# Low parts of weights by adding DMAs, shifted rows for the context's pairs, first modulation in column groups

## Chip, cores and metric

One core of one Trainium2 chip runs the whole kernel. The metric is the device time of one execution in microseconds; the time before is the median of three runs.

## The reference, cut to what matters

Two layers of a hybrid block work on a sequence x of 512 positions and a context of 256 positions, both 1024 wide. Per layer a modulation vector is made from c (for x) and c_ctx (for the context), then each stream is normed, modulated and projected; four branches (retention, short convolution, conformer convolution, windowed attention) are gated and merged.

```python
m = silu(cvec) @ w_mod + b_mod; shift, scale, gate = split(m, 3)
h = rmsnorm(x, norm_w) * (1 + scale) + shift
p = h @ w_in                                   # 1024 -> 11008
r, s, f, a = retention, short conv, conformer conv, attention of p
merged = sum(sigmoid(gate_i) * (branch_i @ w_branch[i]))
x = x + gate * (merged @ w_out)
```

The last layer needs only keys, values and states of the context. After it x is normed once more.

## The kernel before

Everything is kept transposed: features on the 128 partitions, positions along the row, so a stream is 8 blocks (`KC`) of 128 x 512 (x) or 128 x 256 (context). Every large product is done in parts. An operand is split into a high part (rounded to fp32r by a ScalarE copy) and a low part (VectorE: value minus high part), and `mm3` adds three matmuls for each of the 8 blocks: high weight by high data, high weight by low data, low weight by high data. One weight chunk (1024 x 128) is therefore 24 matmuls, moving 256 columns for the context and 512 for x.

The order of work is context of layer 0 (c0), x of layer 0 (x0), keys and values of the context of layer 1 (c1), x of layer 1 (x1), `final`. Within a stream: 54 projection chunks, then 32 gate chunks, each with a branch chunk of 12 matmuls, then 8 output chunks (`mix_out`). TensorE's order is written out by hand; `Tally` holds a planner's costs per engine, and `slot` steps the side flows (retention, attention, convolution taps, norms) between the dense matmuls when the planner says that their inputs are due. The other engines' orders come from the scheduler.

Weights: `w_load` brings a chunk from HBM on SyncE's queue (two 256 KB halves into rows for the context, one 512 KB load into `wraw` for x), `w_split` makes its high and low part in one of three pairs of tiles (`wt`, named wh and wl in the trace), and `w_ahead` keeps two chunks split ahead. The branch weights go into rows of their own (r in the trace). In `w_split`:

```python
nc.scalar.activation(hi, raw, AF.Copy)
nc.vector.tensor_tensor(lo, raw, hi.bitcast(F32), op=ALU.subtract)
```

Rows: `Arena` has 59 rows of 2048 bytes, all starting at a multiple of 64 bytes, and 12 of half that size. Everything that lives longer than an instruction or two is in one: raw weights, activations, splits. A context pair (`pair`, h and l behind the number in the trace) has its two parts in the halves of one row.

Start: `start` does c0's modulation, norm and the first three projections before anything else runs. For each of the 8 blocks, `mod_pe` splits four 128 x 512 tiles of w_mod into high and low part and multiplies them with the four columns of `s4` (high and low of the two silu vectors), `mod_pe_end` adds the four rows and turns them into columns, `modulate` makes the pair of that block, and the dense matmuls of the block follow `LAG` = 3 blocks later.

Of the kernel before, what the change touches and what calls it, by code (L numbers as in the profile page):

```python
# [22 lines left out]
LAG = 3  # L23
# [93 lines left out]
    return c  # L117


NROWS = 59  # L120
PAD = 480


# [28 lines left out]
        self.ring = None  # L152


class Arena:


    def __init__(self, pool, n, nh):
        self.full = [pool.ring(2048, name=f"row{i}") for i in range(n)]
        self.half = [pool.ring(1024, name=f"hrow{i}") for i in range(nh)]  # L160
        self.n = 0

    def get(self, w, parts, keep, pair=False):
        free = self.half if keep and w <= 256 else self.full
        if not free:
            self.relief(free)
# [24 lines left out]
class Tally:  # L191
# [14 lines left out]
    def add(self, eng, op, a, k):  # L206
        aps = [x for x in (*a, *k.values()) if hasattr(x, "free_size")]
        out, src = aps[0], aps[1] if len(aps) > 1 else aps[0]
        n = src.free_size()
        ready = max([self.now, self.read.get(out.tensor.name, 0.0)] + [self.written.get(x.tensor.name, 0.0) for x in aps])  # L210
        if eng == "tensor":
            if op == "transpose":
                d = 0.109
            elif aps[2].dtype == F32:
                d = max(0.218, aps[2].free_size() / 600)
            else:
                d = aps[2].free_size() / 2400
                if aps[2].dtype == F32R and d < 0.1:
                    d = 0.213
            self.now += d  # L220
            end = self.now + 0.15
        else:
            if eng == "vector":
                d = 0.065 + n / 960
                if op in ("tensor_scalar", "tensor_copy") and n == src.free_size() and "PSUM" not in str(src.space):
                    d = 0.065 + n / 1920
            elif eng == "scalar":
                d = 0.1 + n / 1200
            elif eng == "gpsimd":
# [6 lines left out]
            if eng == "sync":  # L236
# [41 lines left out]
class Block:  # L278
    def __init__(self, ctx, tc, xc, vec, cst, w_a, w_g, w_b, w_o, w_m, out, out2):
# [3 lines left out]
        self.w_m = w_m  # L283

        rp = ctx.enter_context(tc.tile_pool(name="rp", bufs=1))
        rp.tile([P, PAD], F32, name="fill")
        self.arena = Arena(rp, NROWS, 12)
# [4 lines left out]
        self.wt = [[cp.tile([P, 1024], F32R, name=f"w{p}{i}") for p in "hl"] for i in range(3)]  # L292
# [4 lines left out]
        self.vec = cp.tile([P, NV], F32, name="vec")  # L297
# [6 lines left out]
        self.work = [pp.tile([P, 512], F32, name=f"k{i}") for i in range(4)]  # L304
        self.turn = {}
        self.wq, self.wraws, self.wready, self.wkeep = [], [], {}, {}
        self.lanes = [[] for _ in range(5)]
        self.turns = 0
        self.flow = None
# [72 lines left out]
    def get_banks(self, n):  # L382

        while True:
            i = self.turn.get("work", 0)
            ready = max(self.nc.over(self.work[(i + j) % 4]) for j in range(n))
# [38 lines left out]
    def w_load(self):  # L425
# [4 lines left out]
        if small:  # L430
            raws = [(self.row(), slice(o, o + 512)) for o in (0, 512)]
            for r, o in raws:
                nc.sync.dma_start(r.a, src[:, o])
            raws = [(r, r.a, o) for r, o in raws]
        else:
            raw = self.take("wraw")
            nc.sync.dma_start(raw, src)
            raws = [(None, raw, slice(0, 1024))]
        if kind == "g":
            r = self.row()  # L440
            nc.sync.dma_start(r.a, self.wsrc["b"][l, i])
            raws.append((r, r.a, None))
        self.wraws.append((key, raws))

    def w_split(self):
        nc = self.nc
        key, raws = self.wraws.pop(0)
        parts = [self.take("wt")]
        for _, raw, o in raws:
# [78 lines left out]
    def csilu(self):  # L528
# [9 lines left out]
        self.s4 = self.cp.tile([P, KC, 4], F32R, name="s4")  # L538
        nc.scalar.activation(self.s4[:, :, 0:2], self.cs, AF.Copy)
        nc.vector.tensor_tensor(self.s4[:, :, 2:4], self.cs, self.s4[:, :, 0:2].bitcast(F32), op=ALU.subtract)  # L540

    def mod_load(self, l, b, hs=range(4)):

# [12 lines left out]
            if 8 <= m < 16:  # L556
                nc.vector.tensor_scalar(o, o, 1.0, self.v(l, "nw", b, b + 1), op0=ALU.add, op1=ALU.mult)

    def mod_pe(self, tiles):
        nc = self.nc  # L560
        ps = self.bank_now()
        for h, t in enumerate(tiles):
            hi, lo = self.part(), self.part()
            nc.scalar.activation(hi.r, t.a, AF.Copy)
            nc.vector.tensor_tensor(lo.r, t.a, hi.a, op=ALU.subtract)
            for i, x in enumerate((hi, lo)):
                for k in range(2):
                    nc.tensor.matmul(ps[0:4, 0:256], self.s4[:, 2 * h + k], x.r[:, k * 256:k * 256 + 256],
                                     start=(h == 0 and i == 0 and k == 0), stop=(h == 3 and i == 1 and k == 1))
        return ps  # L570

    def mod_pe_end(self, l, b, ps):
        m4 = self.small("m4", [4, 256], 4)
        self.nc.scalar.activation(m4, ps[0:4, 0:256], AF.Copy)
        for j in range(2):
            self.nc.tensor.matmul(ps[:, 256 + 2 * j:258 + 2 * j], m4[:, cs(j)], self.c("sel")[0:4],
                                  start=True, stop=True)
        self.mod_add(l, b, ps[:, 256:], 2)

    def mod_flow(self, l, bs):  # L580
# [755 lines left out]
    def load_x(self, st):  # L1336
        return [self.load_row(st, k) for k in range(KC)]

    def load_row(self, st, k):

        o, w = (0, SEQ) if st.s == 0 else (SEQ, CTX)
        x = self.row(w)
        self.nc.sync.dma_start(x.a, self.xd[st.s][k] if st.l else self.xc[k, :, o:o + w])
        return x

    def start(self, st):

        nc = self.nc
        loads = [self.mod_load(0, 0)]
        st.x = self.load_x(st)  # L1350
        self.csilu()
        acc = None
        for k in range(KC):
            acc = self.square(st.x[k].a, acc)
        names = [("ak", 0), ("av", 0), ("ax", 0)]
        self.early = {}
        ws, pss = [], []
        mods = {}

        def dense(k):  # L1360
            for w, ps in zip(ws, pss):
                self.mm3(ps, w, [None] * k + [st.hx[k]] + [None] * (KC - 1 - k), ks=[k])

        for k in range(KC + LAG):
            if k + 1 < KC:
                loads.append(self.mod_load(0, k + 1))
            if k < 3:
                ws.append(self.w_get("a", st, CIDX[names[k]], False)[0])
                pss.append(self.take("dense")[:, :st.t])
                self.early[st, CIDX[names[k]]] = pss[-1]  # L1370
            if k < KC:
                mods[k] = self.mod_pe(loads.pop(0))
            if 1 <= k <= KC:
                self.mod_pe_end(0, k - 1, mods.pop(k - 1))
            if k == 1:
                res = []
                for _ in self.rms(acc, res):
                    pass
# [6 lines left out]
        st.x = st.rstd = None  # L1385

    def run(self):
        nc = self.nc
# [121 lines left out]
```

## Time and profile before

| | us |
|---|---|
| median of 3 runs (1830.43 to 1831.96) | 1831.37 |
| the profiled execution, its own time | 1828.66 |
| its span in the profile | 1826.9 |

The profile is of one execution. PE is TensorE's matmul row, PEld its weight loads, DVE is VectorE, ACT ScalarE, POOL GpSimd, SP SyncE (SPq its queue of DMA issues). A matmul's record is longer than the distance to the next one, since matmuls are pipelined: the pace is read from start to start. "d<-r81h,wl" reads: output in the PSUM tile d, moving operand r81h, weights wl. The granted TensorE clock is given as a share of the full 2.4 GHz.

### The profile page before, as it was taken

The numbers are of one execution on the slowest core, as the hardware profiler recorded it, in microseconds if no ns is written. First come the engines' busy times: TensorE is split into PE (matmuls) and PEld (weight loads), VectorE is DVE, ScalarE is ACT, GpSimd is POOL, SyncE is SP. The second block draws the span as 40 slices with busy tenths as digits, with TensorE's granted clock in tenths as the row PEclk, the third lists the DMA queues.
The fourth block names the chain that finished last, engine by engine and source line by source line (L and its number), as shares of the span: only waits on it lengthen the run. The fifth ranks groups of instructions, "written<-read, shape, count | busy, mean of one in ns | idle before, by whom it ended". The sixth has DMA issues, their size and how long they took to land. (4 is left out here: it accounts for less than half of the span.)

```text
span 1826.9 us, 27582 instructions
## 1 busy us (share of the span) xinstructions
PE 1798.4 (98%) x10242; PEld 1562.3 (86%) x10242; DVE 1326.9 (73%) x2635; ACT 851.6 (47%) x1625; POOL 27.9 (2%) x34
## 2 busy tenths in 40 slices
PE   6999999999999999999999999999999999999998
PEld 4999999988888888888888889888888888888888
DVE  8899999884556669996998457447999866344445
ACT  6666765553554544423423246445534554323223
POOL 1000000000000000000000000000000000000000
PEclk9999999999999999999999999999999999999999
DMA  9646477743222222233555552322222232332233
GB/s 315 246 129 207 120 239 231 233 138 116 70 70 68 83 81 80 95 113 124 183 167 170 159 190 76 116 70 70 65 92 84 84 95 91 111 105 90 87 116 116
DMA packets 104135, 232.60 MB, mean 127 GB/s; under 512 B 12864, under 2 KB 19776, under 8 KB 104000
## 3 DMA queue, kind: packets, MB, share of 16 engines
q1 hardware_dynamic: 104000, 230.84, 39.1%
q8 instruction: 80, 1.31, 0.3%
q14 instruction: 55, 0.45, 0.1%
HBM read 218.73 MB, written 5.24 MB: 123 GB/s over the span
## 5 line engine op out<-in xcount | busy, mean ns | idle before, releaser
L187 PE MATMUL d<-r,wh 128*128 128x512 f32 (+1 forms) x3136 | 942.8, 383 | 0.3 <-DVE r L187 0.3
L187 PEld LDWEIGHTS d<-r,wh 128*128 128x128 f32 x3136 | 572.7, 188 | 106.2 <-DVE r L187 0.8
L187 PE MATMUL d<-r,wl 128*128 128x512 f32 (+1 forms) x1568 | 597.6, 381 | 0.0
L187 DVE TENSOR_TENSOR wl<-w,wh 128x1024 fp32r<-128x1024 f32 x193 | 235.8, 1222 | 234.7 <-ACT wh L187 228.8
L187 ACT ACTIVATE wh<-w 128x1024 fp32r<-128x1024 f32 x193 | 204.9, 1062 | 412.0 <-PE d L187 354.8
L187 PEld LDWEIGHTS d<-r,wl 128*128 128x128 f32 x1568 | 294.8, 188 | 57.8
L187 ACT ACTIVATE r<-r 128x512 fp32r<-128x512 f32 (+3 forms) x264 | 150.6, 588 | 206.6 <-DVE r L187 93.8
L187 DVE TENSOR_TENSOR r<-r,r 128x512 fp32r<-128x512 f32 (+5 forms) x337 | 207.6, 630 | 33.4 <-ACT r L187 29.5
L187 DVE SCALAR_TENSOR_TENSOR r<-r,h_cfw,r 128x503 f32<-128x503 f32 (+19 forms) x360 | 229.4, 649 | 2.0
L187 PE MATMUL d<-r,r 128*128 128x512 f32 x768 | 184.8, 389 | 0.5 <-DVE r L187 0.5
L187 ACT ACTIVATE wh<-r 128x512 fp32r<-128x512 f32 x208 | 129.2, 630 | 101.7 <-PE d L187 90.0
L187 PEld LDWEIGHTS d<-r,r 128*128 128x128 f32 x768 | 144.1, 188 | 30.8 <-DVE r L187 0.9
L187 DVE TENSOR_TENSOR wl<-r,wh 128x512 fp32r<-128x512 f32 x208 | 140.6, 685 | 18.6 <-ACT wh L187 17.6
L187 DVE SCALAR_TENSOR_TENSOR r<-r,d 128x512 f32<-128x512 f32 (+1 forms) x156 | 92.8, 595 | 55.1 <-PE d L187 32.4
L187 ACT ACTIVATE r<-d 128x512 f32<-128x512 f32 (+2 forms) x234 | 118.5, 507 | 14.1 <-PE d L187 9.5
L187 PE MATMUL k<-r,r 128*128 128x128 f32 (+2 forms) x752 | 112.3, 290 | 2.7 <-ACT p L187 2.6
L187 ACT ACTIVATE r<-k 128x512 fp32r<-128x512 f32 (+4 forms) x162 | 77.0, 523 | 70.2 <-PE k L187 68.7
L187 PEld LDWEIGHTS k<-r,r 128*128 128x128 f32 x752 | 99.5, 191 | 9.0 <-ACT p L187 6.2
L187 ACT ACTIVATE p<-k,s_nm 128x256 f32<-128x256 f32 (+1 forms) x144 | 69.7, 496 | 77.0 <-DVE s_nm L187 76.8
L187 DVE SCALAR_TENSOR_TENSOR r<-r,cs,r 128x256 f32<-128x256 f32 x196 | 83.8, 480 | 1.0 <-DMA r<-w_m 0.4
L187 DVE TENSOR_TENSOR r<-k,r 128x512 fp32r<-128x512 f32 (+2 forms) x88 | 54.5, 653 | 9.2 <-ACT r L187 9.0
L187 ACT ACTIVATE p<-p,s_rc 128x512 f32<-128x512 f32 (+2 forms) x80 | 51.3, 719 | 8.6 <-DVE s_rc L187 8.6
(400 smaller groups left out, 2249.0 us busy)
## 6 DMA issues: line engine op xcount, KB each, us to landing
w<-w_a SPq DMA_DIRECT2D x108, 512.0 KB, 3.5
r<-w_a SPq DMA_DIRECT2D x128, 256.0 KB, 4.8
w<-w_g SPq DMA_DIRECT2D x64, 512.0 KB, 3.5
r<-w_m SPq DMA_DIRECT2D x96, 256.0 KB, 3.8
r<-w_b SPq DMA_DIRECT2D x96, 256.0 KB, 3.3
r<-w_g SPq DMA_DIRECT2D x64, 256.0 KB, 3.7
w<-w_o SPq DMA_DIRECT2D x21, 512.0 KB, 3.5
r<-xc SPq DMA_DIRECT2D x24, 256.0 KB, 3.9
```

Source lines behind the costliest of these rows:

```text
L187: return f(*a, **k)
```

## The change

- Low parts of weights: for x's chunks, and for every second one of the context's, `w_split` no longer subtracts on VectorE. ScalarE writes minus the high part into the low tile, and a DMA issued from GpSimd adds the raw weights to it from HBM. Branch weights stay as they were. `w_ahead` keeps three chunks ahead instead of two, with four pairs of tiles instead of three.
- Rows of two kinds: 36 rows start at a multiple of 64 bytes as before, 22 start 32 bytes behind one. Whole-row parts take the first kind first; context pairs and plain rows take the second kind first. Either takes the other kind when its own is used up.
- First modulation: w_mod's tiles are no longer split. The two silu vectors, padded with zeros to 32 columns, are the weights of 8 plain fp32 matmuls per block, spread over four groups of 32 columns (and 32 output partitions); `mod_pe_end` adds the four groups. Matmuls on zeros (`warm`) stand in the first four blocks.
- Start: six projections instead of three are done in it, in six banks; their weights are split by the old way (`early_weights`), each loaded after the next but one block's tiles. x of the context goes into half rows.
- The planner counts a GpSimd DMA as 1.0 us and its landing like SyncE's.

```diff
 class Arena:
-    def __init__(self, pool, n, nh):
+    def __init__(self, pool, n, odd, nodd, nh):
         self.full = [pool.ring(2048, name=f"row{i}") for i in range(n)]
         self.half = [pool.ring(1024, name=f"hrow{i}") for i in range(nh)]
+        self.odd = [odd.ring(2048, name=f"orow{i}") for i in range(nodd)]
     def get(self, w, parts, keep, pair=False):
-        free = self.half if keep and w <= 256 else self.full
+        if keep and w <= 256:
+            kinds = Kinds([self.half])
+        elif parts and not pair:
+            kinds = Kinds([self.full, self.odd])
+        else:
+            kinds = Kinds([self.odd, self.full])
...
     def w_split(self):
...
             nc.scalar.activation(hi, raw, AF.Copy)
-            nc.vector.tensor_tensor(lo, raw, hi.bitcast(F32), op=ALU.subtract)
+            if o and (not key[3] or self.nsplit % 2):
+                nc.scalar.activation(lo, hi.bitcast(F32), AF.Copy, scale=-1.0)
+                nc.gpsimd.dma_start(lo, src, accum_op=ALU.add)
+            else:
+                nc.vector.tensor_tensor(lo, raw, hi.bitcast(F32), op=ALU.subtract)
-    def w_ahead(self, n=2):
+    def w_ahead(self, n=3):
...
+    def warm(self, n, bank):
+        for _ in range(n):
+            self.nc.tensor.matmul(bank, self.zero[:, :P], self.zero, start=True, stop=True)
+
-    def mod_pe(self, tiles):
+    def mod_pe(self, tiles, warm=None):
         ps = self.bank_now()
-        for h, t in enumerate(tiles):
-            hi, lo = self.part(), self.part()
-            nc.scalar.activation(hi.r, t.a, AF.Copy)
-            nc.vector.tensor_tensor(lo.r, t.a, hi.a, op=ALU.subtract)
-            for i, x in enumerate((hi, lo)):
-                for k in range(2):
-                    nc.tensor.matmul(ps[0:4, 0:256], self.s4[:, 2 * h + k], x.r[:, k * 256:k * 256 + 256],
-                                     start=(h == 0 and i == 0 and k == 0), stop=(h == 3 and i == 1 and k == 1))
+        for k in range(KC):
+            j = 32 * (k % 4)
+            if warm and k == 4:
+                self.warm(*warm)
+            self.nc.tensor.matmul(ps[j:j + 32, 0:256], self.c32[:, k], tiles[k // 2].a[:, k % 2 * 256:k % 2 * 256 + 256],
+                                  start=k < 4, stop=k >= 4)
...
     def start(self, st):
+        names = [("ak", 0), ("av", 0), ("ax", 0), ("ay", 0), ("ax", 1), ("ay", 1)]
+        banks = [b[:, :st.t] for b in self.dense + self.ovs + work[:2]]
...
         for k in range(KC + LAG):
+            dense(min(KC, max(0, k - LAG + 1)))
-            if k + 1 < KC:
-                loads.append(self.mod_load(0, k + 1))
-            if k < 3:
-                ws.append(self.w_get("a", st, CIDX[names[k]], False)[0])
+            if k + 2 < KC:
+                loads.append(self.mod_load(0, k + 2))
+            if k < len(names):
+                ws.append(self.early_weights())
             if k < KC:
-                mods[k] = self.mod_pe(loads.pop(0))
+                self.warm((14, 4, 4, 2)[k] if k < 4 else 0, idle)
+                mods[k] = self.mod_pe(loads.pop(0), (10, idle) if k == 0 else None)
             if 1 <= k <= KC:
                 self.mod_pe_end(0, k - 1, mods.pop(k - 1))
...
             if 1 <= k <= KC:
                 self.modulate(st, k - 1)
-            if k >= LAG:
-                dense(k - LAG)
```

## Rows read from the trace of the kernel before

**Rows 1.** Busy us (count) by stretch: PE, PEld, DVE, ACT, POOL; clock; DMA share; GB/s.

```profile
0.00:10.00 10.00, 2.52 (x12) 1.45 (x13) 5.21 (x29) 5.51 (x12) 1.84 (x5) 1.00 0.78 244
10.00:20.00 10.00, 5.68 (x29) 3.02 (x27) 9.00 (x36) 7.11 (x16) 2.13 (x2) 0.83 0.98 343
20.00:30.00 10.00, 7.38 (x40) 4.02 (x40) 8.61 (x20) 6.38 (x14) 0.93 (x1) 0.83 0.99 351
...
60.00:215.00 155.00, 155.00 (x1294) 154.43 (x1294) 147.80 (x370) 98.67 (x227) 4.08 (x4) 1.00 0.52 169
215.00:365.00 150.00, 150.00 (x1255) 149.83 (x1254) 134.50 (x306) 88.12 (x185) 2.29 (x3) 1.00 0.69 224
385.00:740.00 355.00, 353.43 (x1840) 298.09 (x1839) 233.97 (x464) 172.47 (x346) 5.11 (x5) 1.00 0.27 86
```

**Rows 2.** Who PE waited for between 60 and 1765 us: total, times, longest.

```profile
PE k L187 <- ACT p L187: 3.4, 9, 0.7
PE d L187 <- DVE wl L187: 0.6, 1, 0.6
PE d L187 <- DVE r L187: 0.5, 1, 0.5
```

**Rows 3.** PE in order of time in c0: start, us, instruction.

```profile
63.78 0.28 PE L187 MATMUL d<-r133h,wh 128*128 128x256 f32 x1
...
64.74 0.28 PE L187 MATMUL d<-r51h,wl 128*128 128x256 f32 x1
```

**Rows 4.** PE in order of time, the modulation's matmuls with weights of four columns.

```profile
40.05 1.64 PE L187 MATMUL k<-r,s 128*4 128x256 f32 x13
```

**Rows 5.** PE in order of time in x0's output projection, 512 columns.

```profile
1050.46 0.62 PE L187 MATMUL d<-r,wh 128*128 128x512 f32 x2
...
1055.22 0.62 PE L187 MATMUL d<-r,wh 128*128 128x512 f32 x2
```

**Rows 6.** PE in order of time around one plain fp32 product of 512 columns.

```profile
366.89 1.02 PE L187 MATMUL k<-r,cst 128*128 128x512 f32 x2
...
367.87 0.28 PE L187 MATMUL d<-r580l,wh 128*128 128x256 f32 x1
```

**Rows 7.** DMA in the first 60 us: GB/s in 40 slices; issues, KB each, us to landing.

```profile
GB/s 0 220 159 324 369 356 260 298 265 328 402 403 399 399 396 406 392 247 309 326 130 176 306 283 365 342 374 377 400 406 397 403 403 403 395 399 408 203 61 55
...
r<-w_m SPq DMA_DIRECT2D x32, 256.0 KB, 4.9
```

**Rows 8.** PE in order of time at the end of the start.

```profile
47.54 0.60 PE L187 MATMUL k<-cst,s_m 4*128 4x2 f32 x4
...
51.51 0.38 PE L187 MATMUL d<-r135l,wh 128*128 128x256 f32 x1
...
52.88 0.39 PE L187 MATMUL d<-r51h,wh 128*128 128x256 f32 x1 [0.16 <-ACT r L187]
```

**Rows 9.** Costliest groups: busy us, mean ns of one, idle before.

```profile
L187 DVE TENSOR_TENSOR wl<-w,wh 128x1024 fp32r<-128x1024 f32 x193 | 235.8, 1222 | 234.7 <-ACT wh L187 228.8
L187 ACT ACTIVATE wh<-w 128x1024 fp32r<-128x1024 f32 x193 | 204.9, 1062 | 412.0 <-PE d L187 354.8
...
L187 ACT ACTIVATE wh<-r 128x512 fp32r<-128x512 f32 x208 | 129.2, 630 | 101.7 <-PE d L187 90.0
...
L187 DVE TENSOR_TENSOR wl<-r,wh 128x512 fp32r<-128x512 f32 x208 | 140.6, 685 | 18.6 <-ACT wh L187 17.6
```

**Rows 10.** DVE, 0 to 53 us, by group.

```profile
L187 DVE TENSOR_TENSOR r<-r,r 128x512 fp32r<-128x512 f32 (+1 forms) x39 | 24.2, 637 | 1.4 <-ACT r L187 1.3
```

**Rows 11.** DMA issues, 60 to 215 us: KB each, us to landing.

```profile
r<-w_a SPq DMA_DIRECT2D x75, 256.0 KB, 4.3
...
r<-r SPq DMA_DIRECT2D x32, 32.0 KB, 2.3
```

**Rows 12.** POOL, 53 to 385 us, by group.

```profile
L187 POOL TENSOR_TENSOR s_rsr<-s_ve,cst 128x2 f32<-128x2 f32 x4 | 4.1, 1019 | 151.6 <-DVE s_ve L187 151.6
```

**Rows 13.** DVE over the whole span, one form.

```profile
L187 DVE TENSOR_SCALAR r<-r,s_lmv,s_lrs 128x512 f32<-128x512 f32 x10 | 5.5, 547 | 3.5 <-POOL s_lrs L187 3.2
```

More of the change, by code (lines that the diff above doesn't have):

```diff
@@ L117, in _consts @@
     return c
-NROWS = 59
+NROWS = 36
+NODD = 22
 PAD = 480
@@ L152, in __del__, with __init__, __bool__, first @@
         self.ring = None
+class Kinds:
+    def __init__(self, lists):
+        self.lists = lists
+    def __bool__(self):
+        return any(self.lists)
+    def first(self):
+        return next(x for x in self.lists if x)
 class Arena:
-    def __init__(self, pool, n, nh):
+    def __init__(self, pool, n, odd, nodd, nh):
         self.full = [pool.ring(2048, name=f"row{i}") for i in range(n)]
         self.half = [pool.ring(1024, name=f"hrow{i}") for i in range(nh)]
+        self.odd = [odd.ring(2048, name=f"orow{i}") for i in range(nodd)]
         self.n = 0
     def get(self, w, parts, keep, pair=False):
-        free = self.half if keep and w <= 256 else self.full
-        if not free:
-            self.relief(free)
+        if keep and w <= 256:
[4 more added lines that the diff above has]
+            kinds = Kinds([self.odd, self.full])
+        if not kinds:
+            self.relief(kinds)
+        free = kinds.first()
         ring = free.pop(0)
@@ L228, in add @@
                 d = 0.1 + n / 1200
+            elif eng == "gpsimd" and op == "dma_start":
+                d = 1.0
             elif eng == "gpsimd":
@@ L285, in __init__ @@
         rp = ctx.enter_context(tc.tile_pool(name="rp", bufs=1))
-        rp.tile([P, PAD], F32, name="fill")
-        self.arena = Arena(rp, NROWS, 12)
+        self.vec = rp.tile([P, PAD], F32, name="vec")[:, :NV]
+        ro = ctx.enter_context(tc.tile_pool(name="ro", bufs=1))
+        ro.tile([P, 8], F32, name="fill1")
+        self.arena = Arena(rp, NROWS, ro, NODD, 12)
+        rf = ctx.enter_context(tc.tile_pool(name="rf", bufs=1))
+        rf.tile([P, 504], F32, name="fill2")
         self.arena.relief = self.relief
@@ L291, in __init__ @@
         self.wraw = [cp.tile([P, 1024], F32, name=f"w{i}") for i in range(2)]
-        self.wt = [[cp.tile([P, 1024], F32R, name=f"w{p}{i}") for p in "hl"] for i in range(3)]
+        self.wt = [[cp.tile([P, 1024], F32R, name=f"w{p}{i}") for p in "hl"] for i in range(4)]
         self.pt = [cp.tile([P, 640], F32, name=f"p{i}") for i in range(6)]
@@ L306, in __init__ @@
         self.wq, self.wraws, self.wready, self.wkeep = [], [], {}, {}
+        self.nsplit = 0
         self.lanes = [[] for _ in range(5)]
@@ L385, in get_banks @@
             i = self.turn.get("work", 0)
-            ready = max(self.nc.over(self.work[(i + j) % 4]) for j in range(n))
+            ready = max(self.nc.over(self.work[(i + j) % len(self.work)]) for j in range(n))
             if ready <= self.nc.now or self.flow is None:
@@ L433, in w_load @@
                 nc.sync.dma_start(r.a, src[:, o])
-            raws = [(r, r.a, o) for r, o in raws]
+            raws = [(r, r.a, o, src[:, o]) for r, o in raws]
         else:
@@ L448, in w_split @@
         parts = [self.take("wt")]
-        for _, raw, o in raws:
+        self.nsplit += 1
+        for _, raw, o, src in raws:
             if o is None:
@@ L557, in mod_add @@
                 nc.vector.tensor_scalar(o, o, 1.0, self.v(l, "nw", b, b + 1), op0=ALU.add, op1=ALU.mult)
[L559 to L560 removed]
+    def warm(self, n, bank):
+        for _ in range(n):
+            self.nc.tensor.matmul(bank, self.zero[:, :P], self.zero, start=True, stop=True)
+    def mod_pe(self, tiles, warm=None):
         ps = self.bank_now()
[L562 to L569 removed]
+        for k in range(KC):
[4 more added lines that the diff above has]
+                                  start=k < 4, stop=k >= 4)
         return ps
     def mod_pe_end(self, l, b, ps):
[L573 to L574 removed]
+        m4 = self.small("m4", [P, 256], 4)
+        self.nc.scalar.activation(m4, ps[:, 0:256], AF.Copy)
         for j in range(2):
[L576 to L577 removed]
+            self.nc.tensor.matmul(ps[:, 256 + 2 * j:258 + 2 * j], m4[:, cs(j)], self.c("sel"), start=True, stop=True)
         self.mod_add(l, b, ps[:, 256:], 2)
@@ L1337, in load_x, with load_row, early_weights @@
         return [self.load_row(st, k) for k in range(KC)]
-    def load_row(self, st, k):
+    def load_row(self, st, k, keep=False):
         o, w = (0, SEQ) if st.s == 0 else (SEQ, CTX)
-        x = self.row(w)
+        x = self.row(w, keep)
         self.nc.sync.dma_start(x.a, self.xd[st.s][k] if st.l else self.xc[k, :, o:o + w])
         return x
+    def early_weights(self):
+        nc = self.nc
+        kind, l, i, _ = self.wq.pop(0)
+        ws = []
+        for o in (0, 512):
+            raw = self.row()
+            nc.sync.dma_start(raw.a, self.wsrc[kind][l, i][:, o:o + 512])
+            hi, lo = self.part(), self.part()
+            nc.scalar.activation(hi.r, raw.a, AF.Copy)
+            nc.vector.tensor_tensor(lo.r, raw.a, hi.a, op=ALU.subtract)
+            ws += [(hi, lo, cs(k)) for k in range(4)]
+        return ws
     def start(self, st):
         nc = self.nc
+        names = [("ak", 0), ("av", 0), ("ax", 0), ("ay", 0), ("ax", 1), ("ay", 1)]
+        work = self.work
+        zeros = self.row()
+        nc.gpsimd.memset(zeros.a, 0.0)
+        self.zero = zeros.a.bitcast(BF16)[:, :512]
+        idle = self.ovs[0]
+        banks = [b[:, :st.t] for b in self.dense + self.ovs + work[:2]]
+        self.work = work[2:]
         loads = [self.mod_load(0, 0)]
-        st.x = self.load_x(st)
+        st.x = [self.load_row(st, k, True) for k in range(KC)]
         self.csilu()
@@ L1354, in start, with dense @@
             acc = self.square(st.x[k].a, acc)
[L1355 to L1362, printed above, removed]
-        for k in range(KC + LAG):
-            if k + 1 < KC:
-                loads.append(self.mod_load(0, k + 1))
-            if k < 3:
-                ws.append(self.w_get("a", st, CIDX[names[k]], False)[0])
-                pss.append(self.take("dense")[:, :st.t])
-                self.early[st, CIDX[names[k]]] = pss[-1]
+        loads.append(self.mod_load(0, 1))
+        self.early = {(st, CIDX[x]): b for x, b in zip(names, banks)}
+        ws, done, mods = [], [0] * len(names), {}
+        def dense(blocks):
+            for j, w in enumerate(ws):
+                for k in range(done[j], blocks):
+                    hi, lo, c = w[k]
+                    xh, xl = st.hx[k]
+                    for n, (a, b) in enumerate(((hi, xh), (hi, xl), (lo, xh))):
+                        nc.tensor.matmul(banks[j], a.r[:, c], b.r, start=(k == 0 and n == 0),
+                                         stop=(k == KC - 1 and n == 2))
+                done[j] = max(done[j], blocks)
+        for k in range(KC + LAG):
+            dense(min(KC, max(0, k - LAG + 1)))
[3 more added lines that the diff above has]
+                ws.append(self.early_weights())
             if k < KC:
-                mods[k] = self.mod_pe(loads.pop(0))
+                self.warm((14, 4, 4, 2)[k] if k < 4 else 0, idle)
+                mods[k] = self.mod_pe(loads.pop(0), (10, idle) if k == 0 else None)
             if 1 <= k <= KC:
@@ L1375, in start @@
             if k == 1:
-                res = []
+                res, two = [], self.work
+                self.work = work[:2]
+                self.warm(4, idle)
                 for _ in self.rms(acc, res):
-                    pass
+                    self.warm(4, idle)
+                self.work = two
                 st.rstd = res[0]
@@ L1382, in start @@
                 self.modulate(st, k - 1)
-            if k >= LAG:
-                dense(k - LAG)
-        st.x = st.rstd = None
+            if k == len(names) - 1:
+                self.w_ahead()
+        st.x = st.rstd = self.zero = None
+        self.work = work
+        self.turn["work"] = 2
     def run(self):
```

13 lines of the change are left out of this document (6 added, 7 removed).

## The prediction

> **What bounds it now.** I read the busy table by stretch first, to see which engine never rests. From 60 us on it is PE: 155.00 of 155 and 150.00 of 150 us in the context, 353.43 of 355 in x, at a granted clock of 1.00 [rows 1]. The view of waits, second, has PE wait 3.4 us for ScalarE in the attention between 60 and 1765 us, and 1.1 us for VectorE, 0.6 of it for a low part of weights [rows 2]. So from 60 us on, time is won by a faster pace of the matmuls or not at all. The order of time, third, gives the pace from start to start: 8 steps from 63.78 to 64.74, 0.120 us for 256 columns in the context [rows 3], and 21 steps from 1050.46 to 1055.22, 0.227 us for 512 in x [rows 5]. Fourth, the first 30 us: PE is busy 2.5, 5.7 and 7.4 of each 10, while the DMA stands at 0.98 and 0.99 from 10 us on [rows 1]. The start is held by bytes and then by the splits on VectorE; it ends at 52.88 us, where the fourth projection begins at full pace [rows 8].
>
> **The start.** Six projections are done in it instead of three. Before, the three that follow take 72 x 0.120 = 8.6 us from 52.88 on, so the same work stood at 61.5 us. After, by the order in which `start` asks for them, the sixth projection's weights land last: vec and constants 0.35 MB, w_mod 32 x 256 KB, x 8 x 128 KB, six chunks of 512 KB, together 12.9 MB. The first 18 slices of 1.5 us moved 8.4 MB, and where nothing holds it back the DMA moves 0.40 MB a us [rows 7]: 27 + 4.5/0.40 = 38.3 us. Two split halves, ScalarE 0.63 and VectorE 0.69 each [rows 9], overlap to about 2 us: 40.3. PE then still has 84 dense matmuls (four blocks of the sixth projection, four blocks of all six) = 10.1 us, three ends of modulation at 0.6 [rows 8] and two modulations. A plain fp32 product of 512 columns takes 0.98 us of PE (366.89 to 367.87) [rows 6], so one of 256 about 0.49; eight in four groups cost 0.98 if the groups run beside each other, 3.9 if in turn. I take the first, since the instructions have separate columns and separate outputs: 10.1 + 1.8 + 2.0 = 13.9. The last block's path from the end of its modulation to its pair took 4.0 us before (47.54 to 51.51) [rows 8], and block 6 of all six (2.2 us) covers half: 1.1 to 1.8 of wait. End at 55.5 us, against 61.5: **-6.0 us**. Bounds: -10 if the DMA runs at 0.40 from 5 us on; +2 if the groups run in turn, 2.9 us more for each of two modulations behind the weights and as much again before. The splits of w_mod, 32 of 0.64 on VectorE [rows 10], go. The 46 matmuls on zeros have no row; by the nearest (0.227 for 512 columns) 10 us, at half the clock 21. I put them at nothing because 14 us of PE's first 30 are idle [rows 1] and they stand before waits; the granted clock of 0.83 there can only gain.
>
> Column groups are what the Trainium skill's TensorE: Matmul & The Clock Gate (Packing small matmuls) describes: three groups of 32 columns measured 2.38 times as fast as in turn. By it a block costs some 1.2 to 1.6 us, and the sum would lose about 1 us. No row here shows it.
>
> **The rows.** With weights of four columns 256 moving columns take (1.64 - 0.28)/12 = 0.1135 us [rows 4]; with 128 columns 0.120 [rows 3], and PEld is busy 154.4 of 155 us [rows 1]. In x, where a load is short beside 512 columns, the pace is 0.227 = 2 x 0.1135 [rows 5]. So streaming alone sets 0.1135, and the context loses 0.0065 us a matmul only where a weight load lies beside all of it. Both read rows that start at the same place of a line. That a shift of 32 bytes takes the loss away no row shows: the bounds are 0.120 (nothing; a shifted row of 256 touches one line more, 17 for 16 if a line has 64 bytes, a cost of the same kind as the one that it may remove but a sixteenth of it) and 0.1135. I take 0.1135, because it is the pace of the same rows with the other reader gone, and the difference, 16 cycles at 2.4 GHz for 16 lines, would be one meeting for each such line. The pairs made in the start get shifted rows, since w_mod's rows come back in time: 86 chunks x 24 matmuls, less 144 in the start, are 1920 x 0.0065 = 12.5 us. Branch, output and c1 pairs, 816 matmuls, compete with plain rows for 22; half of them give 2.7. **-15 us**, from 0 to -18. x's whole-row parts stay on lines, so x's pace stays.
>
> The trace speaks against the Trainium skill here: SBUF — State Buffer (Who interferes with whom) gives PE two independent read ports, for the moving operand and the weights, and its 16-byte lines (Specifications) make 32 bytes a whole number of lines. By both, the shift is worth nothing and the sum would be -6.
>
> **The low parts.** Removed from VectorE: 193 x 1.222 and 98 x 0.685 = 303 us; added to ScalarE: 193 x 1.062 and 98 x 0.63 = 267 us [rows 9]; added to GpSimd: 291 DMA issues, 127 MB read twice. VectorE is at 95% in the context and yet PE lost nothing there [rows 1]; relief alone gains at most the 1.1 us of PE's waits for VectorE [rows 2]. But it is the cover of the second part: at 0.1135 the context is 6% shorter, and VectorE's 282 us of 305 would hardly fit; now they fall by 67. ScalarE gets 62 us on top of its 187 of 305 there, and in x at most 1.062 for each chunk of 24 x 0.227 us, 19 points on top of 49% [rows 1, 9]. PE's waits for it, 3.4 us [rows 2], may double. I set relief against that: **0**, from -1 to +6. In front of a GpSimd DMA that waits for its copy stand, on the same queue, the `pow`s of the norms, 1.0 us each, 4 of retention in the context [rows 12]; who waits is a side flow, not a dense matmul.
>
> Is a low part there in time? A pair of tiles is free when PE ends a chunk and needed three chunks later. In the context that is 72 x 0.1135 = 8.2 us; the chain is two copies of 0.63, about 1.0 for ScalarE's other work (64% busy), GpSimd's issue at 1.0 (its nearest row [rows 12]) and the landing. The nearest landing, 256 KB by SyncE in this stretch, is 4.3 us, the fastest 2.3 [rows 11]; an adding DMA also reads what it writes, so twice 4.3 is the upper end. At 4.3 the chain is 7.6 and fits, by 0.6 us. In x the time is 72 x 0.227 = 16.3, in the context's gates 108 x 0.1135 = 12.3: both fit even at 8.6. I take 4.3, as the bytes per partition and the engines are the same.
>
> Sum: -6 - 15 + 0 = -21: the profiled execution's 1828.66 becomes 1807.7. It lies 2.7 us under the median of the runs, so the time is 1831.4 - 21 = **1810**.
>
> **Rivals.** *The shift does nothing* (or the pairs don't get the rows): for it, no row has a shifted operand; against it, 0.120 beside 0.1135. 1831.4 - 6 = 1825. *Column groups run in turn*: 1831.4 + 2 - 15 = 1818; for it, no row shows any two matmuls side by side. *Low parts come late*, the one on the slower side: place, the context's projections after the start, 48 chunks, 24 of them by DMA. It decides from a landing of 4.9 us on, where the chain passes 8.2. At 8.6 the chain is 11.9, and as three chunks must last that long, two take 7.9 instead of 5.45: 24 x 2.5 = 60 us. At 6.5 the chain is 9.8, two take 6.5, 25 us: 1835. So slower than before above some 6.2, up to 1870; I put it at 1848. For it: DMA share 0.52 and 0.69 there before the added bytes [rows 1], and four copies in a burst on ScalarE. Against it: half a chunk's slack for the second half. The Trainium skill names a cause: SBUF — State Buffer (The "DVE blocks DMA" trap) says that GpSimd can't write descriptors while VectorE runs a two-port operation. By row, one-input operations of 512 take 0.547 us [rows 13] and are few, so I give that little.
>
> **Numbers.** My forecast 0.55 (own range 1798 to 1819), shift idle 0.17, groups in turn 0.11, low parts late 0.17. Two in ten may be left out: I leave out most of the last and gains beyond the bounds, 1797 to 1836. A change under 0.2%, 3.7 us, can't be told from none. Faster: 0.54 + 0.14 + 0.11 = 0.79; same: 0.01 + 0.03 + 0.02 = 0.06; slower 0.15.
>
> **What would show it.** Start: sixth projection's end near 55 us, splits of w_mod gone. Rows: context pace 0.1135 instead of 0.120 at pairs in shifted rows. Low parts: VectorE some 320 us less busy, ScalarE some 250 more, PE's waits for wl under 2 us. I am wrong if the context's pace stays at 0.120, if the view of waits has PE behind a DMA into wl, or if PE's waits for ScalarE grow past 10 us.

## The result and the profile after

The changed kernel takes 1959.5 us (median of four runs, 1950.97 to 1961.5) against 1831.1: a ratio of 1.0692, 95% interval 1.066 to 1.0724. It is 128 us slower; 1810 us were forecast. Its profiled execution has a span of 1956.8 us.

First the busy table by stretch, which answers to [rows 1]; the columns are the same.

```profile
20.00:30.00 10.00, 7.01 (x32) 3.90 (x32) 6.31 (x21) 2.38 (x6) 0.00 (x0) 0.58 0.64 225
...
60.00:215.00 155.00, 124.05 (x965) 120.28 (x965) 107.19 (x277) 92.11 (x214) 32.94 (x38) 0.91 0.81 199
215.00:365.00 150.00, 132.98 (x1066) 129.60 (x1065) 85.36 (x197) 95.46 (x207) 30.52 (x36) 0.97 0.86 227
385.00:740.00 355.00, 333.25 (x1908) 292.61 (x1908) 159.52 (x380) 210.71 (x380) 51.97 (x59) 0.96 0.73 176
```

PE, never idle before, is idle for 31 and 17 us in the context's two stretches, and the granted clock falls with it. VectorE and ScalarE are *less* busy per microsecond than before in the first stretch: no engine there is full, and PE waits. When x's first projection begins, at 486.3 us instead of 391.6, 94.7 of the 129.9 us of the two profiles are lost; so most of the loss lies in layer 0's context. The DMA share rises from 0.52 and 0.69 to 0.81 and 0.86, while the bytes grow far less (169 to 199 GB/s, 224 to 227).

The queues on the page (packets, MB, share of 16 engines) say where the share goes: GpSimd's queue, all adding transfers, takes a larger share than SyncE's with little more than half of its bytes.

```profile
q0 software_dynamic: 41904, 126.90, 39.0%
q1 hardware_dynamic: 104000, 230.84, 35.6%
```

The waits of PE from 60 to 1765 us, as in [rows 2], which held 4.5 us:

```profile
PE d L210 <- DVE r L210: 18.6, 8, 4.6
PE d L210 <- DMA wl<-w_a: 13.9, 8, 8.2
PE k L210 <- DVE r L210: 13.2, 5, 7.8
PE d L210 <- ACT r L210: 11.3, 6, 3.6
PE k L210 <- DVE s_nm L210: 10.8, 2, 9.4
PE k L210 <- ACT p L210: 8.5, 13, 2.5
```

DMA issues from 60 to 215 us (KB each, us to landing); before, the raw rows landed after 4.3 and the small copies after 2.3 [rows 11]:

```profile
r<-w_a SPq DMA_DIRECT2D x68, 256.0 KB, 4.8
wl<-w_a POOLq DMA_DIRECT2D x34, 256.0 KB, 6.6
r<-r SPq DMA_DIRECT2D x40, 32.0 KB, 5.2
```

One late low part in order of time, from 68 to 80 us, shows the whole chain:

```profile
68.12 0.63 ACT L210 ACTIVATE wh<-r 128x512 fp32r<-128x512 f32 x1 [3.70 <-DMA r<-w_a]
...
70.64 0.63 ACT L210 ACTIVATE wh<-r 128x512 fp32r<-128x512 f32 x1 [0.54 <-DMA r<-w_a]
71.18 0.61 ACT L210 ACTIVATE wl<-wh 128x512 fp32r<-128x512 f32 x1
...
72.08 1.78 POOL L210 DMA_DIRECT2D wl<-w_a  x2 [10.12 <-ACT r L210]
...
80.05 0.58 PE L210 MATMUL d<-r48h,wl 128*128 128x256 f32 x1 [8.22 <-DMA wl<-w_a]
```

ScalarE stands behind a raw load, so its copies are late, so GpSimd's issue at 72.08 is late, and PE waits 8.22 us for the landing. Two things are late here, the raw row and the low part. The experiments ask which of them is the cause and which only follows.

### The profile page after: what moved, and what is told of

It is laid out like the page before. It is cut to its first block, busy times and chain, and to the rows that moved or that the text cites. A ratio compares the mean times of both kernels' runs of the same rounds, so it can differ in the third digit from the quotient of the medians.

```text
span 1956.8 us, 28161 instructions
## 1 busy us (share of the span) xinstructions
PE 1843.3 (94%) x10286; PEld 1585.8 (81%) x10288; DVE 1044.3 (53%) x2312; ACT 1061.8 (54%) x1883; POOL 280.1 (14%) x327
## 4 chain that ended last, share of the span: by engine, by line
PE 62%; DMA 15%; DVE 10%; ACT 6%; issue 5%; SPq 1%; POOL 1%; ACTq 0%; DVEq 0%; POOLq 0%
PE d L210 53%; DVE r L210 8%; PE k L210 8%; DMA r<-w_a 4%; DMA r<-w_b 3%; ACT r L210 2%; DMA r<-xc 2%; ACT wh L210 2%; PE ov L210 2%; DMA r<-w_m 2%; ACT p L210 1%; DMA r<-r 1%; SPq L210 1%; DMA wl<-w_a 1%; ACT wl L210 1%
## 5 line engine op out<-in xcount | busy, mean ns | idle before, releaser
L210 PEld LDWEIGHTS d<-r,wl 128*128 128x128 f32 x1568 | 296.8, 189 | 63.9 <-DMA wl<-w_o 4.4
L210 DVE TENSOR_TENSOR r<-r,r 128x512 fp32r<-128x512 f32 (+5 forms) x317 | 194.8, 628 | 196.9 <-ACT r L210 194.2
L210 ACT ACTIVATE r<-r 128x512 fp32r<-128x512 f32 (+3 forms) x244 | 139.6, 585 | 283.1 <-DMA r<-w_b 119.8
L210 ACT ACTIVATE wl<-wh 128x1024 fp32r<-128x1024 f32 (+1 forms) x291 | 264.6, 910 | 2.6
L210 POOL DMA_DIRECT2D wl<-w_a x166 | 144.7, 873 | 831.8 <-ACT wl L210 672.8
L210 DVE SCALAR_TENSOR_TENSOR r<-r,h_cfw,r 128x503 f32<-128x503 f32 (+15 forms) x360 | 231.4, 651 | 5.1
L210 POOL DMA_DIRECT2D wl<-w_g x96 | 83.1, 875 | 587.1 <-ACT wl L210 442.5
L210 ACT ACTIVATE wh<-r 128x512 fp32r<-128x512 f32 x196 | 120.1, 624 | 84.2 <-DMA r<-w_a 32.2
L210 DVE TENSOR_TENSOR wl<-r,wh 128x512 fp32r<-128x512 f32 x98 | 66.9, 687 | 56.5 <-ACT wh L210 52.3
L210 ACT ACTIVATE r<-k 128x512 fp32r<-128x512 f32 (+5 forms) x164 | 77.4, 519 | 25.0 <-PE k L210 22.0
```

What stands on the lines that cost most here:

```text
L210: return f(*a, **k)
```

## Experiments

Theory 1: adding transfers are late, and ScalarE's queue, which keeps its order, stands behind late loads. Rivals: ScalarE's second copies; the rows of two kinds; the start. The kernel before took 1830.1 to 1830.9 us beside each of the groups below.

**Which part.** In the first four the order of the work was held as in the changed kernel: the planner still saw its operations. Low parts by VectorE:

```diff
-                nc.scalar.activation(lo, hi.bitcast(F32), AF.Copy, scale=-1.0)
-                nc.gpsimd.dma_start(lo, src, accum_op=ALU.add)
...
+                nc.vector.engine.tensor_tensor(lo, raw, hi.bitcast(F32), op=ALU.subtract)
```

> All low parts by VectorE again, with the order of all work, the rows and the start as in the changed kernel. Theory 1 (adding transfers are late, ScalarE waits in its queue behind late loads): nearly all of the 128 us comes back, about 1825 us (start +3, shift of rows some -2 to -12). Rival: rows of two kinds, the longer lead or the new order of the work cost the time: it stays above 1900.

Measured 1912.1 (ratio 1.0443, 1.0423 to 1.0463): 47 us back, 82 not. Theory 1 in its first form falls: most of the loss is there without one adding transfer. But this order was made for a VectorE with less to do, so the run doesn't yet convict the rows.

The same with the transfers kept in x alone, `if key[3]` going to VectorE:

> Adding transfers only in x (every chunk), the context's low parts by VectorE, order as in the changed kernel. Theory 1: x has 16 us for a low part, so it loses only what the trace shows from x's gates on (about 30 us): 1825 + 30 = 1855 us. Rival (context and x are late for the same reason, bytes): x holds two thirds of the adding bytes and loses two thirds, about 1910.

Measured 1900.9 (1.0368 to 1.0412), and kept in the context alone, `if not key[3]` going to VectorE:

> Adding transfers only for every second chunk of the context, x's low parts by VectorE, order as in the changed kernel. Theory 1: the first 400 us lose as in the changed kernel (about 95 us), the rest runs as before: 1920 us. Rival (bytes, spread evenly): about 1860.

Measured 1975.0 (1.077 to 1.0809). Neither expectation was met, but the two differ by 74 us: under this order transfers in x cost nothing (11 us less than without any) and those in the context, with a fifth of the added bytes (98 halves of 256 KB beside 193 chunks of 512 KB), cost 63.

Both copies on ScalarE, and VectorE adding instead of the transfer:

```diff
-                nc.gpsimd.dma_start(lo, src, accum_op=ALU.add)
...
+                nc.vector.engine.tensor_tensor(lo, raw, lo.bitcast(F32), op=ALU.add)
```

> ScalarE still makes both copies of each chunk that went by transfer, and VectorE adds the raw weights to the second copy; no adding transfers. Theory 1 (the transfers): within 10 us of the kernel with all low parts by VectorE, about 1830. Rival 2 (265 us more work on ScalarE are what PE waits for): within 20 us of the changed kernel, about 1940.

Measured 1918.3 (1.0465 to 1.05): 6 us over the run without the copies. ScalarE's added work is not the cause of the 128 us.

**Rows and start, with orders of their own.** VectorE's subtractions throughout, three pairs of weight tiles, two chunks of lead:

```diff
-NROWS = 36
+NROWS = 40
...
-            if o and (not key[3] or self.nsplit % 2):
+            if False:
...
-    def w_ahead(self, n=3):
+    def w_ahead(self, n=2):
```

> Low parts by VectorE, one chunk of lead and one pair of weight tiles less (40 + 22 rows), rows of two kinds and the new start kept, and an order of work made for just these operations. The 1912 us with the changed kernel's order had few waits on weights but long ones at the joins of the stages. Theory 2 (an order made for operations that the engines don't run costs that; rows and start are sound): start +3 by the trace, shift -2.3 ns for each of some 1900 matmuls = -4: about 1830. Rival (rows of two kinds, fewer of them, or the new start cost by themselves): 1880 or more.

Measured 1873.9 (1.0221 to 1.0249). The rival was nearer: 43 us are lost with an order that fits and no adding transfer. The second kind of rows on a whole 64 bytes (`fill1` of 16 columns):

> The same kernel and order, but the second kind of rows moved by 32 bytes on to a whole 64 bytes. Theory (the shift takes 2 to 3 ns from a matmul of 256 columns): 4 to 6 us slower than with the shift. My forecast's figure (6.5 ns) would make it 12 to 15 us slower. Rival (nothing): equal.

Measured 1874.4 (1.021 to 1.0253): 0.5 us apart, though single executions of the second ran from 1864.7 to 1877.0. By the traces PE has a mean of 116.8 ns for 256 columns with 32 bytes and 117.7 with 64 (60 to 224 us), so this pair compares two shifts, and not a shift with none. And the start alone (`NROWS = 60`, `NODD = 0`):

> The kernel before with the new start alone (60 plain rows, low parts by VectorE, two chunks of lead, its own order). By the changed kernel's trace the start is 3 us late: 1834. Rival (that start was held up by the added transfers' waits, and by itself gains what I forecast): 1825.

Measured 1858.6 (1.0139 to 1.0167), off both. The cause was mine, as the same kernel without them shows below: two fillers of 64 bytes had put the weight tiles 128 bytes further, and x's matmuls of 512 columns took 231 to 232.5 ns. PE in order of time in x (start, us, instruction):

```profile
599.68 0.39 PE L210 MATMUL d<-r,wl 128*128 128x512 f32 x1
...
601.76 0.39 PE L210 MATMUL d<-r,wl 128*128 128x512 f32 x1
```

9 steps in 2.08 us are 0.231, where [rows 5] had 0.227. The accident became an experiment (below).

**How a row is chosen.** What had not been looked at was the list. Before, a free row was the one that had been free longest. Now `Kinds.first` empties the short shifted list first, so a load gets a row that was given back only a little earlier in the order of the program, and whose last reader may not have run. In the 1874 us kernel ScalarE's waits in the context's gates (232 to 394 us; total, times, longest) are:

```profile
ACT r L210 <- DMA r<-w_b: 29.9, 19, 3.7
ACT wh L210 <- DMA r<-w_g: 27.1, 12, 5.9
ACT wh L210 <- PE d L210: 4.4, 3, 1.6
```

```diff
         free = kinds.first()
+        if not (keep and w <= 256) and not parts:
+            free = min((x for x in kinds.lists if x), key=lambda x: x[0][0])
...
```

> The 1874 us kernel (low parts by VectorE, rows of two kinds, new start), but a load or a plain result takes the row that has been free longest, of either kind, instead of always one of the shifted kind. Theory (a row that has just been given back in the order of the program is still being read, and SyncE's queue waits for its reader, so loads come late): 1831 - 1 (start, 60.5 against 61.5 in the trace of the start alone) - 5 (3 ns for each of some 1650 context matmuls) = 1825. Rival (that there are two kinds at all, or how the start is built): 1865 to 1874.

Measured 1832.4 (1.0001 to 1.002): 41.5 us from one edit of the choice, with PE's order of work unchanged. The same view, same stretch, of this kernel:

```profile
ACT r L228 <- DMA r<-w_b: 14.6, 6, 4.1
...
ACT wh L228 <- PE d L228: 11.2, 16, 1.2
```

The copies of w_g now wait for PE to free their tiles, that is, they are early; no line for w_g's landing is left among the largest. From 60 to 365 us SyncE's queue waited 175.2 us for VectorE to be done with rows and low parts in the 1874 us kernel, and 128.3 us in this one. The same edit in the changed kernel:

> The changed kernel, with nothing else altered than that a load or plain result takes the row that has been free longest. If the choice of rows costs it what it costs the kernel without adding transfers, some 45 us come back: 1915. Rival (loads are late because of the adding transfers, and rows are held by these): 1945 or more.

Measured 1879.8 (1.0247 to 1.0281): 80 us of the 128 are the choice of rows, nearly twice what was expected. That late rows also delay adding transfers can be only a part of the reason: with plain transfers in the same order, the next two runs, the same edit takes off 63.9 us.

**What an adding transfer costs.** Plain transfers in place of the adding ones (the low parts then hold the weights themselves), with the changed kernel's choice of rows:

```diff
-                nc.gpsimd.dma_start(lo, src, accum_op=ALU.add)
+                nc.gpsimd.dma_start(lo, src.bitcast(F32R))
```

> The changed kernel with plain transfers in the place of the adding ones, so the low parts hold the weights themselves; copies, queue and order as in it. If adding is what keeps the DMA engines twice as long for a byte, the GpSimd queue's share falls from 39% to some 20%, the landing from 6.1 us to some 4, and the time falls by a good part of the 47 us between the changed kernel and the one with VectorE's subtractions in its order: 1915 to 1930. Rival (the queue or the wait for ScalarE's copy, not the adding): 1950 or more.

Measured 1910.8 (1.0422 to 1.0451), just under its range. It is also what VectorE's subtractions took in this order with these rows (1912.1): adding apart, the way through ScalarE and GpSimd and the second reading cost nothing here. The same with longest-free rows:

> The kernel of 1880 us (adding transfers, longest-free rows) with plain transfers in place of the adding ones; low parts hold the weights themselves. Theory 1 (an adding transfer keeps the DMA engines about twice as long for a byte, which fills them to 0.93 in the context and makes low parts late): share in the context falls to 0.7 to 0.75, and most of the 47 us over the 1832 us kernel come back, 1840. Rival (ScalarE's second copy and the long way through ScalarE and GpSimd are what is late): 1865 or more.

Measured 1846.9 (1.0082 to 1.0113), against 1879.8 with adding: 33 us. The queue's line on the page, with adding:

```profile
q0 software_dynamic: 41904, 126.90, 40.4%
```

and with plain transfers:

```profile
q0 software_dynamic: 41904, 126.90, 23.6%
```

The same packets and bytes keep the engines 1.7 times as long when they add. From 60 to 215 us (columns as in [rows 1]), with adding:

```profile
60.00:215.00 155.00, 144.39 (x1202) 142.10 (x1201) 116.30 (x300) 109.57 (x251) 40.35 (x45) 0.99 0.93 244
```

and with plain ones:

```profile
60.00:215.00 155.00, 150.26 (x1265) 149.13 (x1264) 123.12 (x313) 120.74 (x273) 28.43 (x49) 0.99 0.80 256
```

The share falls from 0.93 to 0.80 while more bytes move; the expected 0.7 to 0.75 was not reached, and 14.5 us remain to the 1832.4 of the kernel without transfers. That rest (the longer way through two queues, the second reading, 36 rows instead of 40, three chunks of lead with a fourth pair of tiles, another order) was not split further; the pair at 1910.8 and 1912.1 speaks for the rows, the lead and the order.

Adding transfers in x alone, on top of the 1832.4 us kernel:

```diff
-            if False:
+            if o and not key[3]:
```

> As the first of this call (longest-free rows, 40 + 22 rows, two chunks of lead), with x's low parts by adding transfers. Theory (x has time enough, and PE waits for nothing there anyway): within 5 us of the first, about 1825. Rival (two chunks of lead, 11 us, are too few for copies, issue and a landing of 6 us): PE behind wl, 1840 or more.

Measured 1867.9 (1.0188 to 1.0216): the rival. PE's waits over the whole span:

```profile
PE d L228 <- DMA wl<-w_o: 14.1, 6, 5.7
PE k L228 <- ACT p L228: 13.0, 11, 4.3
PE d L228 <- DMA wl<-w_a: 6.8, 3, 4.2
```

With two chunks of lead even x has no room for them, and the output projection (w_o) least. With three, in the changed kernel's order, they cost nothing in x (1900.9 against 1912.1); no run changes the lead alone.

**The start and the turns.** The start alone, without my fillers:

> The kernel with the new start alone once more, without two fillers of 64 bytes that had put its weight tiles 128 bytes behind the rows' places (modulo 2 KB). In its trace x's matmuls of 512 columns took 231 to 232.5 ns on the mean instead of 227.5; 4600 of them make 20 us. Theory (weights and rows at unequal places cost 512 columns that): 1830. Rival (the start's other order slows x): 1855 again.

Measured 1841.7 (1.0036 to 1.0063). x's matmuls are at 227 ns again and 17 us are back, but 11 remain, nearly all of them past 390 us. There the order has changed: of the 1328 matmuls into k, which belong to side flows, 974 stand at another place among x's big ones in the trace. The new start takes three projections, and with them three turns, out of the loop that lets the side flows in by rotation. With the turns added:

```diff
         self.turn["work"] = 2
+        self.turns += 3
```

> The kernel with the new start alone (1842 us), with the same 3 turns added. Theory: 1842 - 10 = 1831, the start itself being worth nothing (its first new projection after the six began at 62.0 us, the same work stood at 61.5 before). My forecast's start (-6) would make it 1825. Rival: 1842.

Measured 1834.4 (1.0013 to 1.003); 52 of 1328 have moved now, and 7 us are back. PE's waits for the attention's `p` from 60 to 1765 us, without the turns,

```profile
PE k L210 <- ACT p L210: 9.7, 16, 3.1
```

and with them, nearer to the 3.4 us of [rows 2]:

```profile
PE k L210 <- ACT p L210: 5.3, 12, 1.0
```

What is left is +3.7 us. The new start ends at 61.63 us, where the same work stood at 61.5; when x begins the profiled execution is 1.2 us late, and the rest comes in x, where its cause is open.

**The shift.** The kernel before with rows of two kinds alone (`Kinds`, the two pools, the longest-free choice):

```diff
-NROWS = 59
+NROWS = 40
+NODD = 22
```

> The kernel before with rows of two kinds alone (40 + 22, longest-free row for loads), its own start, all low parts by VectorE. The kernel with the new start and these rows takes 1832, the one with the new start alone 1842: theory (the shift takes 3 ns from a matmul of 256 columns whatever the start): 1830 - 9 = 1821 to 1826, faster than the kernel before. Rival (the 9 us between those two are a difference in the order of the work): 1830.

Measured 1827.5 (0.9976 to 0.9994), 2.9 us under the kernel before, and less than the 4 to 9 expected. New start, shift and turns together (the longest-free kernel with `self.turns += 3`):

> The 1832 us kernel (new start, rows of two kinds with the longest-free choice, low parts by VectorE) with the counter of the planner's turns set on by 3, for the three projections that the new start takes out of the loop; the side flows then have their turns as in the kernel before, and x's small matmuls stand where they stood (40 of 1233 moved instead of 828). Theory (the 7 to 10 us that x loses with the new start come from that other order): 1832 - 8 = 1824, faster than the kernel before. Rival (x loses them by something else in the start): 1832.

Measured 1824.2 (0.9948 to 0.9973): 6.6 us under the kernel before, the fastest of all. PE in order of time in its context:

```profile
99.79 0.28 PE L228 MATMUL d<-r60h,wl 128*128 128x256 f32 x1
...
101.19 0.28 PE L228 MATMUL d<-r102h,wl 128*128 128x256 f32 x1
```

12 steps in 1.40 us are 0.1167, against 0.120 [rows 3]. Last, the kernel before with its weight tiles 32 bytes further and nothing else:

```diff
+        rf = ctx.enter_context(tc.tile_pool(name="rf", bufs=1))
+        rf.tile([P, 8], F32, name="fill2")
         self.cp = cp = ctx.enter_context(tc.tile_pool(name="cp", bufs=1))
```

> The kernel before with one edit, a filler of 32 bytes ahead of the weight tiles; order, rows and operations are untouched. Theory (what counts is where a matmul's weights and moving row lie to each other, not that a row is shifted): the context's 256 columns fall from 120 to 117 ns, 3264 x 3 = -10 us, and x's 512 columns rise from 227 to 234, 4600 x 7 = +32 us: 1852. Rival (rows off a line by themselves): no change, 1830.

Measured 1849.4 (1.0083 to 1.0114). PE in x:

```profile
599.71 0.40 PE L187 MATMUL d<-r,wl 128*128 128x512 f32 x1
...
603.91 0.40 PE L187 MATMUL d<-r,wl 128*128 128x512 f32 x1
```

18 steps in 4.20 us are 0.233, against 0.227 [rows 5]. No row is shifted here, and still 512 columns slow down; 256 columns ran at 118.3 ns on the mean from 62 to 224 us, against 119.9 before, and x began 2.4 us earlier. So, for these shifts, it is where weights and moving row lie to each other that counts, and it counts the other way round for 256 and for 512 columns.

## Why the prediction was wrong

The runs make a chain from the kernel before to the changed one: 1830.8; +3.7 for the new start with its turns kept; -10.3 for the shift; +8.2 for the lost turns; +14.5 for low parts by plain transfers, with 36 rows, three chunks of lead and another order; +32.9 for adding; +79.7 for the choice of rows; 1959.5. Each step is a difference between two measured kernels, and its size hangs on what stands beside it: the choice of rows is 41.5 without transfers and 63.9 with plain ones, and adding is 48.7 where the choice of rows is the changed kernel's.

- **The rows: the step that failed.** I costed the two kinds by PE's pace alone: "The pairs made in the start get shifted rows, since w_mod's rows come back in time". That the edit takes every other user's row from the shifted list first, so that loads stop getting the row that is free longest, has no term in the sum and no rival. It is the largest part, 42 to 80 us, and 68 of the 80 are lost in layer 0's context (x begins at 418.2 us with the longest-free choice, at 486.3 without).
- **The shift** was the right mechanism with a mis-sized term: 0.1167 us instead of the 0.1135 that I took, half of the gain. Between pairs of kernels that differ by it, it measured 9.3 and 10.3 us on the new start, against 15 forecast, but 2.9 on the old one. The traces show most of why. From the fourth projection on the old start (52.88 us) and from the seventh on the new one (61.63) to the beginning of x, shifted rows gain 5.9 and 6.2 us, so there the two agree. But the old start with these rows ends 4.2 us later, at 57.09 instead of 52.88; from 20 to 40 us its clock is 0.57 and 0.58, where the kernel before has 0.83 [rows 1] and 1.00:

```profile
20.00:30.00 10.00, 7.57 (x34) 4.63 (x35) 7.79 (x21) 8.16 (x18) 0.70 (x1) 0.57 1.05 394
30.00:40.00 10.00, 9.71 (x49) 6.67 (x47) 7.37 (x19) 5.38 (x13) 0.00 (x0) 0.58 0.69 268
```

The 10.3 holds some 4 us more that are gained in x at an unchanged pace; why is open. The Trainium skill's SBUF — State Buffer (Who interferes with whom) gives PE one read port for the moving operand and an independent one for the weights, by which moving either is worth nothing; the trace disagrees, in x with 0.233 against 0.227, and the measurement decides.
- **The low parts**: "I take 4.3" for the landing. It was 6.6 from 60 to 215 us, past the 6.2 above which my rival ends slower. With the rows out of the way the transfers cost 47 us (14.5 + 32.9), and 28 of them are there when x begins (418.2 against 390.2 us), in the rival's place and within its 25 to 60. Its mechanism, PE behind a DMA into wl, is there with 10.1 us in 7 waits from 60 to 400 us, not with all 28. I gave it 0.17 because I took 4.3. I had the second reading as an upper end of the landing only, and not as engine time that raw loads then lack: those land later too, 4.8 against 4.3 and 5.2 against 2.3 [rows 11], and ScalarE stands behind them; with plain transfers in the same order and rows both land after 4.1.
- **The engines' loads** were near: VectorE 1326.9 to 1044.3 us, 283 less for 320 forecast, ScalarE 851.6 to 1061.8, 210 more for 250, on the pages; the copies themselves cost 6 us.
- **The start**: the column groups do run beside each other. In the changed kernel, at a granted clock of 1.00, PE has

```profile
38.58 1.07 PE L210 MATMUL k<-r,c 128*32 128x256 f32 x16
```

1.07 us, near the 0.98 that I took and far from 3.9. What failed is the time at which the sixth projection's weights are split, 40.3 us in the sum. In the fastest kernel VectorE ends that split at 47.90:

```profile
46.61 1.29 DVE L228 TENSOR_TENSOR r<-r,r 128x512 fp32r<-128x512 f32 x2
```

Its weights were asked for at 33.95 us, and loads asked for then landed after 5.0 us (the median), so they were there near the 38.3 of the sum. But ScalarE, whose copies come first, takes them up at 45.96 only: the split stands in its queue behind a block's modulation, for which it waited 2.41 us for PE and 1.29 for VectorE. From 47.90 on the sum holds: 13.6 us to the next projection's first matmul, for 13.9 and a wait of 1.1 to 1.8.

```profile
61.53 0.28 PE L228 MATMUL d<-r48h,wh 128*128 128x256 f32 x1
```

The same work stood at 61.5 before, so the start gains nothing. "The granted clock of 0.83 there can only gain" failed too. Up to 26 us the clock is 1.00, but then PE, waiting for splits and without a filler from 21.8 to 29.5 us, is nearly idle, and it falls (columns as in [rows 1]):

```profile
24.00:26.00 2.00, 0.09 (x1) 0.09 (x1) 1.90 (x12) 1.17 (x3) 0.00 (x0) 1.00 1.03 391
26.00:28.00 2.00, 0.88 (x4) 0.47 (x4) 1.28 (x3) 1.09 (x3) 0.00 (x0) 0.92 1.05 392
28.00:30.00 2.00, 1.75 (x4) 0.88 (x5) 1.27 (x2) 0.55 (x1) 0.00 (x0) 0.50 1.05 387
...
36.00:38.00 2.00, 2.00 (x18) 0.63 (x17) 0.00 (x0) 0.00 (x0) 0.00 (x0) 0.52 1.04 396
38.00:40.00 2.00, 2.00 (x20) 1.92 (x16) 1.06 (x4) 0.46 (x2) 0.00 (x0) 1.00 1.05 396
```

From 28 to 38 us PE is busy all but 0.25 us, at 0.50 or little more, which is 1.2 GHz. One such block of eight products, 1.07 us above, takes 1.94 us there. So the lower clock may hold some 5 of the 7.6 us by which the split is late; that is an estimate from these rows, and no run took the lower clock away.

- **The order of the work** has no term in the sum either: three turns fewer are 7 to 8 us in x.

## What to carry to other kernels

A pool that hands out the buffer free longest hides waits that no profile of it shows; an edit that prefers one kind of buffer must be costed as a change of every load's wait, not only of the operand that it moves. An engine's share of DMA time is the budget for new transfers, not the bytes: an adding one counted 1.7 times here, and in a queue that keeps its order a late load delays all behind it. With an order made by a planner, look whether the order has moved before a difference is put down to the hardware.

## What the runs showed of the hardware

- Adding transfers of 126.9 MB took 40.4% of the DMA engines' time in one kernel, plain ones of the same packets 23.6%. GpSimd was busy for 0.87 us with the issue of an adding one and for 0.53 us with that of a plain one.
- 256 columns of fp32r with 128 weight columns took 0.120 us with weights and row at equal places modulo 2 KB and 0.1167 with the row 32 bytes further; 512 columns took 0.227 at equal places, 0.231 with the weights 128 bytes further and 0.233 with 32. (Places are where weight tile and row start.)
- Moved by 64 bytes instead of 32, the rows gave the same time within the interval (1874.4 and 1873.9 us).
- One block of eight plain fp32 products of 256 columns, in four groups of 32 weight columns, took 1.07 us at a granted clock of 1.00. In the fastest kernel the clock stood at 0.50 from 28 to 38 us, after PE had been busy for 0.97 of the 4 us before.
